# Feed-forward values, residual stream and softmax turned by VectorE and DMA moves in an encoder trunk

## The chip, the cores and the metric

The kernel runs on one core of a Trainium2 chip. The metric is the device time of one execution in microseconds (us), as the median of several runs. All data are float32. The engines of the core are PE (TensorE, matmuls), ACT (ScalarE), DVE (VectorE), POOL (GpSimd) and SP (SyncE, which here only issues DMAs).

## The reference

The input x has 256 tokens of 2048 features; two layers are followed by a last RMSNorm. A layer is:

```python
h    = rms_norm(x, norm1_w)
proj = h @ w_in                       # q, k, v, z, xbc, dt, u
att  = dilated_window_attention(...)  # 3 dilations x 8 slots of 64, merged by their softmax denominators
ssd  = ssd_mixer(...)                 # bidirectional chunked scan, gated, normed: 1024 channels
pool = multiscale_pool(u, ...)        # 512 channels
x    = x + concat(att, ssd, pool) @ w_out
h    = rms_norm(x, norm2_w)
x    = x + (silu(h @ w_gate) * (h @ w_up)) @ w_down     # 5632 inner features
```

## The kernel before

**Units.** The weights (one long array, wall) are cut into 421 units of at most 128x2048 floats, 1 MB. The main loop goes over the units, one step for each. A unit is either of the feature kind (mm_feature: weights stationary, the result has features on the partitions: dt, xbc, q and k, u) or of the token kind (mm_token: the activations stationary, the result has tokens on the partitions: z, v, out, gate, up, down). A token result of 512 columns takes four units (q = 0 to 3), a down result as many as the part has blocks.

**Precision.** Each product is made of float32r pairs. prep splits a weight half (128x1024) into hi (ACT cast, L148) and lo (DVE, L149); the activations are kept as such pairs too (tiles xp, mix, ffp). A token unit has 24 matmuls of 512 columns on PE.

**Order.** All is issued in an order written out by hand, and each engine executes its instructions in that order. In step i SP issues the load of unit i+2 (`load(i + RAW_AHEAD)`, three raw buffers); then the work planned for position "a" is issued; then ACT and DVE prepare the halves 2i+3 and 2i+4 (unit i+1's second and unit i+2's first; five buffers for halves, so a half's buffer is free when PE has used the half five before it); then the work at "b"; then evac takes the result of unit i-1; then the work at "c"; then PE's matmuls of unit i, between which the work planned for a position k of 0 to 15 is put (run_side, side_slot). In a token unit the positions 4kk to 4kk+3 all come at the start of the group kk. `at(step, fn, ..., pos=...)` plans a piece of work.

**What is turned today.** PE turns a 128x128 piece by an instruction of its own, into a PSUM bank, from which ACT and DVE take it. Three places of this kind are touched:

- ff_trans: the feed-forward values (tokens on the partitions), eight transposes for each of 11 blocks of 512 features in a layer, into the pairs ffp (features on the partitions) that the down product reads. Blocks are grouped in parts of 4, 4 and 3 (PARTS); after each part comes its down product.
- xtrans_feat: the residual stream xs after out and after the last down, eight for each of four blocks, into the pairs xp of the next products; three times in the kernel.
- att_b: the softmax (att_a scores and exponent, att_n the scaling), 128x512 for each head slot and token half, eight for a pair and half; att_c multiplies with v. There are four pairs in each layer.

```python
at(b + c, att_a, pair, c, pos=13)
at(b + c + 1, att_n, pair, c, pos="a")
for sl in range(2):
    at(b + c + 1, att_b, pair, sl, c, pos=5)
at(b + c + 2, att_c, pair, c, pos=2)
```

The small transposes of the scan (dt_cols, xtrans, gate2) aren't touched. Tiles t2 are 128x512 (38 buffers), tiles t3 128x768 (8 buffers).

Of the kernel before, what the change touches and what calls it, by code (L numbers as in the profile page):

```python
# [15 lines left out]
F32 = mybir.dt.float32  # L19
F32R = mybir.dt.float32r  # L20
AF = mybir.ActivationFunctionType
ALU = mybir.AluOpType
# [25 lines left out]
def trunk(ctx, tc, xT, xin, wall, par, fin, dsk, plw, cst, dtab, rcnt, out):  # L48
# [22 lines left out]

    def t3(name, dt=F32):
        return ep.tile([128, 3, T], dt, tag="e", name=name)

    def bank(name):
        return auxp.tile([128, 512], F32, tag="aux", name=name)
# [114 lines left out]
    def xpair(k, l, off, v=None):  # L191
# [6 lines left out]
        DVE.scalar_tensor_tensor(t[:, T:], v, w, t[:, :T].bitcast(F32), op0=ALU.mult, op1=ALU.subtract)  # L198
        st["xp"][k] = t

    def residual(n, accs):
        for c in range(2):
            x = xs[c][:, n * 512:n * 512 + 512]
            DVE.tensor_tensor(x, x, accs[c], op=ALU.add)
# [5 lines left out]
            q = t2("sq")  # L210
            ACT.activation(q, xs[c][:, n * 512:n * 512 + 512], AF.Square, accum_out=st["ssq"][:, c * 4 + n:c * 4 + n + 1])

    def xtrans_feat(n, l, off, half):
        p = bank("xf")
        for b in range(2):
            f = (4 * n + 2 * half + b) * 128
            for c in range(2):
                PE.transpose(p[:, b * T + c * 128:b * T + c * 128 + 128], xs[c][:, f:f + 128], ident)  # L218
                yield
        for b in range(2):  # L220
            xpair(4 * n + 2 * half + b, l, off, p[:, b * T:b * T + T])

    def rstd_cols():
        r = sm.tile([128, T + 4], F32, name="rbc", bufs=1)
# [418 lines left out]
    def att_a(pair, c):  # L643
        q, k = st["qk", pair, 0], st["qk", pair, 1]
        p = [bank("sc") for _ in range(2)]
        for o, n, m in ((0, T, 0), (T, 128, 1), (T + 128, 128, 2)):
            for sl in range(2):
                a = slice(64 * sl, 64 * sl + 64)
                PE.matmul(p[sl][:, o:o + n], lhsT=q[a, m, c::2], rhs=k[a, m] if m == 0 else k[a, m, c::2],  # L649
                          start=True, stop=True)  # L650
        if c == 1:
            del st["qk", pair, 0], st["qk", pair, 1]
        for sl in range(2):
            s = t2("s")
            mx = sm.tile([128, 4], F32, tag="mx", name="mx", bufs=6)
            DVE.tensor_tensor_reduce(s, p[sl], dtb[:, c], scale=SLOT_D[2 * pair + sl], scalar=-3e38, op0=ALU.add,  # L656
                                     op1=ALU.max, accum_out=mx[:, 0:1])
            DVE.tensor_scalar(mx[:, 1:2], mx[:, 0:1], -1.0, None, op0=ALU.mult)
            ACT.activation(s, s, AF.Exp, bias=mx[:, 1:2], accum_out=mx[:, 2:3])
            st["p", pair, sl, c] = (s, mx)  # L660

    def att_n(pair, c):
        for sl in range(2):
            s, mx = st["p", pair, sl, c]
            DVE.reciprocal(mx[:, 3:4], mx[:, 2:3])
            DVE.tensor_scalar(s, s, mx[:, 3:4], None, op0=ALU.mult)
            st["p", pair, sl, c] = s

    def att_b(pair, sl, c):
        s = st["p", pair, sl, c]  # L670
        p = bank("pt")
        for b in range(4):
            PE.transpose(p[:, b * 128:b * 128 + 128], s[:, b * 128:b * 128 + 128], ident)  # L673
            yield
        t = t2("pts")
        ACT.copy(t, p)
        st["p", pair, sl, c] = t

    def att_c(pair, c):
        if c == 0:  # L680
            st["op", pair] = bank("op")
        p = st["op", pair]
        pt = [st.pop(("p", pair, sl, c)) for sl in range(2)]
        vs = (st["v", 0, 0], st["v", 0, 1], st["v", 1, c], st["v", 2, c])
        for b in range(4):
            for sl in range(2):
                h = (2 * pair + sl) * 64
                PE.matmul(p[64 * sl:64 * sl + 64, c * 128:c * 128 + 128], lhsT=vs[b][:, h:h + 64],  # L688
                          rhs=pt[sl][:, b * 128:b * 128 + 128], start=(b == 0), stop=(b == 3))
        del pt  # L690
        if c == 0:
            return
        del st["op", pair]
        t = t2("mix", F32R)
        pv = p[:, :T].rearrange("p (c j) -> p j c", c=2)
        hv = t[:, :T].rearrange("p (j c) -> p j c", c=2)
        lv = t[:, T:].rearrange("p (j c) -> p j c", c=2)
        ACT.copy(hv, pv)
        DVE.tensor_tensor(lv, pv, hv.bitcast(F32), op=ALU.subtract)
        st["mix"][MIX_ATT[pair]] = t  # L700
        if pair == 3:
            for g in range(3):
                for c in range(2):
                    del st["v", g, c]
# [41 lines left out]
    def ff_up(f, accs):  # L746
        st["fv"] = []
        for c in range(2):
            v = t2("fv")
            DVE.scalar_tensor_tensor(v, accs[c], st["r"][:, T + c:T + c + 1], st["sg"][c], op0=ALU.mult, op1=ALU.mult)  # L750
            st["fv"].append(v)
        del st["sg"]

    def ff_trans(f, half, fv):
        p = bank("ft")
        for b in range(2):
            o = (2 * half + b) * 128
            for c in range(2):
                PE.transpose(p[:, b * T + c * 128:b * T + c * 128 + 128], fv[c][:, o:o + 128], ident)  # L759
                yield  # L760
        for b in range(2):
            t = t2("ffp", F32R)
            v = p[:, b * T:b * T + T]
            ACT.copy(t[:, :T], v)
            DVE.tensor_tensor(t[:, T:], v, t[:, :T].bitcast(F32), op=ALU.subtract)
            st["ff", 4 * f + 2 * half + b] = t

    def fin_load():
        st["fw"] = [t2("fw") for _ in range(4)]
# [27 lines left out]
    def evac(i, acc):  # L797
# [43 lines left out]
        elif kind == "v":  # L841
            if j % 4 == 3:
                v_evac(j // 4, acc)
        elif kind == "qk":
            pair, m = divmod(j, 6)
            qk_evac(pair, m, acc)
            if m == 5:
                b = i + 3 if pair == 0 else i + 2
                for c in range(2):
                    at(b + c, att_a, pair, c, pos=13)  # L850
                    at(b + c + 1, att_n, pair, c, pos="a")
                    for sl in range(2):
                        at(b + c + 1, att_b, pair, sl, c, pos=5)
                    at(b + c + 2, att_c, pair, c, pos=2)
        elif kind == "u":
            if j == 3:
                pass
            pool_evac(j, acc)
            at(i + 2, pool_mm, l, j, pos=11)
        elif kind == "out":  # L860
            residual(j, acc)
            squares(j)
            at(i + 2, xtrans_feat, j, l, P_N2, 0, pos=2)
            at(i + 2, xtrans_feat, j, l, P_N2, 1, pos=10)
            if j == 3:
                at(i + 3, rstd_cols, pos="b")
        elif kind == "gate":
            st["sg"] = []
            for c in range(2):
                s = t2("sg")  # L870
                ACT.activation(s, acc[c], AF.Silu, scale=st["r"][:, T + c:T + c + 1])
                st["sg"].append(s)
        elif kind == "up":
            ff_up(j, acc)
            fv = st.pop("fv")
            at(i + 2, ff_trans, j, 0, fv, pos=2)
            at(i + 2, ff_trans, j, 1, fv, pos=10)
        elif kind == "down":
            residual(j, acc)
            if u["part"] == len(PARTS) - 1:  # L880
                squares(j)
                if l + 1 < L:
                    at(i + 2, xtrans_feat, j, l + 1, P_N1, 0, pos=2)
                    at(i + 2, xtrans_feat, j, l + 1, P_N1, 1, pos=10)
                    if j == 3:
                        at(i + 3, rstd_cols, pos="b")
                        at(i + 4, rstd_rows, pos=2)
                        at(i + 5, rstd_parity, pos=2)
                else:
                    if j == 0:  # L890
                        ACT.activation(warm, epst, AF.Sqrt)
                        fin_load()
                    if j < 3:
                        fin_weight(j)
            if j == 3:
                for f in range(4 * u["f0"], 4 * (u["f0"] + u["nq"])):
                    del st["ff", f]
# [51 lines left out]
def _constants():  # L949
# [18 lines left out]
    s = np.arange(T)  # L968
    n = [np.minimum(s + w // 2, T) - np.maximum(s - w // 2, 0) for w in (2, 4, 8, 16)]
    rc = (1.0 / np.stack(n)).astype(np.float32).reshape(2, 512)  # L970
    return c, d.astype(np.float32), rc


def _feature(w):
# [9 lines left out]
def _pack(inp):  # L984
    out = []
    put = lambda a: out.append(np.ascontiguousarray(a).reshape(-1))
    for l in range(L):
        w = inp["w_in"][l]
        q, k, v, z, xbc, dt, u = np.split(w, np.cumsum([ATT, ATT, ATT, INNER, 1536, 32])[:6], axis=1)
        put(_token(z))  # L990
        dtp = np.zeros((D, 128), np.float32)
# [18 lines left out]
        for n in range(HELD):  # L1010
            put(o[n][3])
        put(o[HELD:])
        g, up = _token(inp["w_gate"][l]), _token(inp["w_up"][l])
        gu = np.stack([g, up], axis=1)
        f0 = 0
        for n in PARTS:
            put(gu[f0:f0 + n])
            put(_token(inp["w_down"][l][f0 * 512:(f0 + n) * 512]))
            f0 += n
    return np.concatenate(out)  # L1020

# [36 lines left out]
```

## Time and profile before

| | |
|---|---|
| median of 3 runs | 2465.73 us (2465.63 to 2467.09) |
| the profiled execution: its time | 2464.96 us |
| its span, from the first to the last instruction | 2463.2 us |
| PE busy | 2440.2 us, 99% of the span |
| DVE, ACT, POOL busy | 1427.1, 1186.4, 238.1 us (58%, 48%, 10%) |
| mean granted TensorE clock | 0.998 of full speed |
| DMA moved | 458.57 MB, 186 GB/s over the span |

PE's busy time counts latencies of overlapping instructions, so the cost of one matmul is read from the distance of starts. In the rows L149 is line 149 of the kernel; "out<-in" are the program's names; SPq is SP's queue of DMA issues.

### The profile page before, as it was taken

The numbers are of one execution on the slowest core, as the hardware profiler recorded it, in microseconds if no ns is written. First come the engines' busy times: TensorE is split into PE (matmuls) and PEld (weight loads), VectorE is DVE, ScalarE is ACT, GpSimd is POOL, SyncE is SP. The second block draws the span as 40 slices with busy tenths as digits, with TensorE's granted clock in tenths as the row PEclk, the third lists the DMA queues.
The fourth block names the chain that finished last, engine by engine and source line by source line (L and its number), as shares of the span: only waits on it lengthen the run. The fifth ranks groups of instructions, "written<-read, shape, count | busy, mean of one in ns | idle before, by whom it ended". The sixth has DMA issues, their size and how long they took to land.

```text
span 2463.2 us, 30214 instructions
## 1 busy us (share of the span) xinstructions
PE 2440.2 (99%) x11954; PEld 2029.4 (82%) x11954; DVE 1427.1 (58%) x1791; ACT 1186.4 (48%) x1610; POOL 238.1 (10%) x329
## 2 busy tenths in 40 slices
PE   8999999999999999999999999999999999999997
PEld 7888888888888888888888888888888888888886
DVE  6787765555454555545558787655545545454454
ACT  6576554544444444344555755445544444444443
POOL 2175002000000000000001830020000000000001
PEclk9999999999999999999999999999999999999999
DMA  7565544455555555555454654445555555555553
GB/s 271 200 220 171 175 153 155 172 204 188 188 188 196 193 185 194 189 188 190 173 201 157 225 180 155 165 160 188 187 190 188 188 193 187 194 193 191 188 200 125
DMA packets 67103, 458.57 MB, mean 186 GB/s; under 512 B 7776, under 2 KB 7920, under 8 KB 13328
## 3 DMA queue, kind: packets, MB, share of 16 engines
q1 hardware_dynamic: 63360, 445.27, 50.6%
q0 software_dynamic: 3456, 11.09, 1.6%
q8 instruction: 94, 1.54, 0.3%
q14 instruction: 49, 0.40, 0.0%
q10 hardware_dynamic: 144, 0.26, 0.0%
HBM read 454.43 MB, written 2.16 MB: 185 GB/s over the span
## 4 chain that ended last, share of the span: by engine, by line
PE 98%; DVE 1%; ACT 0%; issue 0%; DMA 0%; POOL 0%; SPq 0%; DVEq 0%; ACTq 0%; POOLq 0%
PE acc L321 25%; PE acc L324 25%; PE acc L322 25%; PE acc L286 11%; PE acc L288 6%; PE ft L759 1%; PE acc L291 1%; PE sc L649 1%; PE op L688 1%; PE pt L673 1%; PE y L569 0%; PE y L567 0%; PE xf L218 0%; DMA raw<-wall 0%; DVE s L656 0%
## 5 line engine op out<-in xcount | busy, mean ns | idle before, releaser
L149 DVE TENSOR_TENSOR wlo<-raw,whi 128x1024 fp32r<-128x1024 f32 (+1 forms) x839 | 1028.0, 1234 | 846.9 <-ACT whi L148 845.7
L148 ACT CAST whi<-raw 128x1024 fp32r<-128x1024 f32 (+1 forms) x839 | 873.5, 1049 | 976.9 <-PE acc L324 832.9
L321 PE MATMUL acc<-whi,xp 128*128 128x512 f32 x1728 | 685.8, 397 | 8.4 <-ACT whi L148 8.4
L324 PE MATMUL acc<-whi,xp 128*128 128x512 f32 x1728 | 685.5, 397 | 0.0
L322 PE MATMUL acc<-wlo,xp 128*128 128x512 f32 x1728 | 674.8, 391 | 0.0
L286 PE MATMUL acc<-xp,whi 128*128 128x512 f32 x1230 | 458.3, 409 | 0.0
L321 PEld LDWEIGHTS acc<-whi,xp 128*128 128x128 f32 x1728 | 326.0, 189 | 77.5 <-ACT whi L148 8.4
L324 PEld LDWEIGHTS acc<-whi,xp 128*128 128x128 f32 x1728 | 326.0, 189 | 70.9
L322 PEld LDWEIGHTS acc<-wlo,xp 128*128 128x128 f32 x1728 | 326.2, 189 | 63.6 <-DVE wlo L149 0.4
L288 PE MATMUL acc<-xp,wlo 128*128 128x256 f32 x1312 | 367.2, 290 | 0.0
L324 PE MATMUL acc<-whi,ffp 128*128 128x512 f32 x704 | 277.3, 394 | 0.0
L321 PE MATMUL acc<-whi,ffp 128*128 128x512 f32 x704 | 277.3, 394 | 0.0
L322 PE MATMUL acc<-wlo,ffp 128*128 128x512 f32 x704 | 274.1, 389 | 0.0
L286 PEld LDWEIGHTS acc<-xp,whi 128*128 128x128 f32 x1230 | 231.3, 188 | 50.4 <-issue 3.2
L288 PEld LDWEIGHTS acc<-xp,wlo 128*128 128x128 f32 x1312 | 248.2, 189 | 14.5 <-issue 0.8
L324 PEld LDWEIGHTS acc<-whi,ffp 128*128 128x128 f32 x704 | 132.2, 188 | 29.5
L321 PEld LDWEIGHTS acc<-whi,ffp 128*128 128x128 f32 x704 | 132.2, 188 | 28.6
L322 PEld LDWEIGHTS acc<-wlo,ffp 128*128 128x128 f32 x704 | 132.3, 188 | 26.2
L451 POOL TENSOR_TENSOR pad<-cd,rbc 128x256 f32<-128x256 f32 x24 | 18.7, 781 | 1019.8 <-DVE cd L274 1019.8
L324 PE MATMUL acc<-whi,mix 128*128 128x512 f32 x256 | 102.7, 401 | 0.0
L321 PE MATMUL acc<-whi,mix 128*128 128x512 f32 x256 | 102.1, 399 | 0.0
L322 PE MATMUL acc<-wlo,mix 128*128 128x512 f32 x256 | 99.8, 390 | 0.0
(183 smaller groups left out, 1584.1 us busy)
## 6 DMA issues: line engine op xcount, KB each, us to landing
raw<-wall SPq DMA_DIRECT2D x417, 1024.0 KB, 4.8
rowb<-rowd POOLq DMA_DIRECT2D x32, 256.0 KB, 3.7
xt<-xT SPq DMA_DIRECT2D x8, 256.0 KB, 7.7
xs<-xin SPq DMA_DIRECT2D x2, 1024.0 KB, 7.9
out<-xs SPq DMA_DIRECT2D x5, 256.0 KB, 3.4
raw<-wall SPq DMA_DIRECT2D x4, 256.0 KB, 5.9
rc<-rcnt POOLq DMA_DIRECT2D x4, 256.0 KB, 5.8
fw<-fin POOLq DMA_DIRECT2D x4, 256.0 KB, 3.6
```

Of the source, the lines that this page charges most:

```text
L148: ACT.copy(hi[:, c:e], r)
L149: DVE.tensor_tensor(lo[:, c:e], r, hi[:, c:e].bitcast(F32), op=ALU.subtract)
L286: PE.matmul(acc, lhsT=hi, rhs=rhs, start=first, stop=False)
L288: PE.matmul(acc[:, T:], lhsT=lo, rhs=rhs[:, :T], start=False, stop=False)
L291: PE.matmul(acc, lhsT=hi, rhs=rhs, start=False, stop=True)
L321: PE.matmul(a, lhsT=xh, rhs=hi[:, s], start=first, stop=False)
L322: PE.matmul(a, lhsT=xh, rhs=lo[:, s], start=False, stop=False)
L324: PE.matmul(a, lhsT=xl, rhs=hi[:, s], start=False, stop=last)
L649: PE.matmul(p[sl][:, o:o + n], lhsT=q[a, m, c::2], rhs=k[a, m] if m == 0 else k[a, m, c::2], start=True, stop=True)
L673: PE.transpose(p[:, b * 128:b * 128 + 128], s[:, b * 128:b * 128 + 128], ident)
L688: PE.matmul(p[64 * sl:64 * sl + 64, c * 128:c * 128 + 128], lhsT=vs[b][:, h:h + 64], rhs=pt[sl][:, b * 128:b * 128 + 128], start=(b == 0), ...
L759: PE.transpose(p[:, b * T + c * 128:b * T + c * 128 + 128], fv[c][:, o:o + 128], ident)
```

## The change

The three kinds of PE transposes are taken out. In their place VectorE turns a 128x512 block in 32x32 pieces (each piece in its place), and 16 DMAs on SP's queue, each 32 partitions by 128 columns, move the pieces between the partition groups (`move`). The order of features within 512 is permuted by this; the rows of w_in, w_gate, w_up and w_down, the two norm weights, the transposed input and the distance table are permuted on the host to fit, and the scores are written to PSUM in the permuted order. The hi and lo parts are then taken from the moved tile in SBUF with a strided view (`turned`), one 128x128 piece at a time, so each of these lines has twice as many instructions of half the size. The moves are issued at position "a" two steps after the unit that made the values; the splits stand at positions 2 and 8 of the same step; att_b moves to the step of att_c, and att_c from position 2 to 10.

```diff
+    def move(v, d):
+        for a in range(4):
+            for b in range(4):
+                nc.sync.dma_start(d[32 * b:32 * b + 32, 128 * a:128 * a + 128],
+                                  v[32 * a:32 * a + 32, 128 * b:128 * b + 128])
+
+    def turned(d, m):
+        return d.rearrange("p (a m j) -> p m a j", a=4, m=4)[:, m]
...
-    def xtrans_feat(n, l, off, half):
-        p = bank("xf")
-        for b in range(2):
-            f = (4 * n + 2 * half + b) * 128
+    def x_turn(n):
+        st["xv", n] = [t3f("xv") for _ in range(2)]
+        for c in range(2):
+            DVE.transpose(st["xv", n][c], xs[c][:, n * 512:n * 512 + 512])
+
+    def x_move(n):
+        st["xd", n] = [t2("xd") for _ in range(2)]
+        for v, d in zip(st.pop(("xv", n)), st["xd", n]):
+            move(v, d)
+
+    def x_split(n, l, off, half):
...
+        for m in (2 * half, 2 * half + 1):
+            k = 4 * n + m
+            t = t2("xp", F32R)
+            w = pr[:, l, off + k:off + k + 1]
             for c in range(2):
-                PE.transpose(p[:, b * T + c * 128:b * T + c * 128 + 128], xs[c][:, f:f + 128], ident)
-                yield
-        for b in range(2):
-            xpair(4 * n + 2 * half + b, l, off, p[:, b * T:b * T + T])
+                v = turned(st["xd", n][c], m)
+                hi, lo = (cols(t[:, o + c * 128:o + c * 128 + 128]) for o in (0, T))
+                ACT.activation(hi, v, AF.Copy, scale=w)
+                DVE.scalar_tensor_tensor(lo, v, w, hi.bitcast(F32), op0=ALU.mult, op1=ALU.subtract)
+            st["xp"][k] = t
...
-        for o, n, m in ((0, T, 0), (T, 128, 1), (T + 128, 128, 2)):
+        for o, n, m in ((0, 2, 0), (2, 1, 1), (3, 1, 2)):
...
-                PE.matmul(p[sl][:, o:o + n], lhsT=q[a, m, c::2], rhs=k[a, m] if m == 0 else k[a, m, c::2],
-                          start=True, stop=True)
+                PE.matmul(p[sl].rearrange("p (b m i) -> p m b i", b=4, m=4)[:, o:o + n], lhsT=q[a, m, c::2],
+                          rhs=k[a, m] if m == 0 else k[a, m, c::2], start=True, stop=True)
...
             DVE.tensor_scalar(s, s, mx[:, 3:4], None, op0=ALU.mult)
+            DVE.transpose(s, s)
...
-    def att_b(pair, sl, c):
-        s = st["p", pair, sl, c]
-        p = bank("pt")
-        for b in range(4):
-            PE.transpose(p[:, b * 128:b * 128 + 128], s[:, b * 128:b * 128 + 128], ident)
-            yield
-        t = t2("pts")
-        ACT.copy(t, p)
-        st["p", pair, sl, c] = t
+    def att_b(pair, c):
+        for sl in range(2):
+            d = t3f("pts")
+            move(st["p", pair, sl, c], d)
+            st["p", pair, sl, c] = d
...
-            st["fv"].append(v)
+            t = t3f("ft")
+            DVE.transpose(t, v)
+            st["fv"].append(t)
...
+    def ff_move(f):
+        st["fd"] = [t2("fd") for _ in range(2)]
+        for v, d in zip(st.pop("fv"), st["fd"]):
+            move(v, d)
...
-                    for sl in range(2):
-                        at(b + c + 1, att_b, pair, sl, c, pos=5)
-                    at(b + c + 2, att_c, pair, c, pos=2)
+                    at(b + c + 2, att_b, pair, c, pos="a")
+                    at(b + c + 2, att_c, pair, c, pos=10)
...
-            at(i + 2, ff_trans, j, 0, fv, pos=2)
-            at(i + 2, ff_trans, j, 1, fv, pos=10)
+            at(i + 2, ff_move, j, pos="a")
+            at(i + 2, ff_split, j, 0, pos=2)
+            at(i + 2, ff_split, j, 1, pos=8)
```

ff_split is built as x_split, without the weight; x_turn is called behind squares, x_move and x_split are planned as ff_move and ff_split are.

## Rows read from the trace of the kernel before

**Rows 1.** The profile's page: first line of the chain that ended last.

```profile
PE 98%; DVE 1%; ACT 0%; issue 0%; DMA 0%; POOL 0%; SPq 0%; DVEq 0%; ACTq 0%; POOLq 0%
```

**Rows 2.** Groups by line and form: count, busy us, mean ns, idle before.

```profile
L759 PE MATMUL ft<-cs,fv 128*128 128x128 f32 x176 | 47.7, 271 | 0.0
...
L673 PE MATMUL pt<-cs,s 128*128 128x128 f32 x128 | 32.3, 273 | 1.8 <-DVE s L666 1.8
...
L218 PE MATMUL xf<-cs,xs 128*128 128x128 f32 x96 | 26.0, 271 | 0.0
...
L507 ACT COPY xs<-xt 128x128 f32<-128x128 f32 x16 | 4.1, 256 | 6.1 <-PE xt L504 6.1
```

**Rows 3.** Timeline of PE, starts of three gate units: start us, us.

```profile
903.45 0.39 PE L321 MATMUL acc<-whi,xp 128*128 128x512 f32 x1
...
909.86 0.39 PE L321 MATMUL acc<-whi,xp 128*128 128x512 f32 x1
...
915.30 0.39 PE L321 MATMUL acc<-whi,xp 128*128 128x512 f32 x1
```

**Rows 4.** Timeline of PE, last matmuls of feature units in the attention, and att_c.

```profile
300.72 0.40 PE L291 MATMUL acc<-xp,whi 128*128 128x512 f32 x1
...
307.67 0.40 PE L291 MATMUL acc<-xp,whi 128*128 128x512 f32 x1
...
315.48 0.40 PE L291 MATMUL acc<-xp,whi 128*128 128x512 f32 x1
...
316.50 1.09 PE L688 MATMUL op<-pts,v 128*64 128x128 f32 x16
```

**Rows 5.** Timeline of DVE: the scaling of the softmax.

```profile
308.81 0.49 DVE L666 TENSOR_SCALAR s<-s,mx 128x512 f32<-128x512 f32 x1
```

**Rows 6.** Timeline of DVE and ACT after an up block.

```profile
900.43 1.40 DVE L750 SCALAR_TENSOR_TENSOR fv<-acc,rbc,sg 128x512 f32<-128x512 f32 x2
...
904.73 1.23 DVE L149 TENSOR_TENSOR wlo<-raw,whi 128x1024 fp32r<-128x1024 f32 x1 [1.49 <-ACT whi L148]
...
903.64 1.05 ACT L148 CAST whi<-raw 128x1024 fp32r<-128x1024 f32 x1 [1.66 <-PE acc L324]
```

**Rows 7.** Timeline of SP's queue at the start.

```profile
2.12 1.85 SPq L131 DMA_DIRECT2D raw<-wall  x4
4.02 0.91 SPq L158 DMA_DIRECT2D xt<-xT  x2
...
5.55 2.53 SPq L158 DMA_DIRECT2D xt<-xT  x2
```

**Rows 8.** Issues of the weight loads: duration ns, least, median, most.

```profile
L133 SPq DMA_DIRECT2D raw<-wall x417: 327/328/538, 5.0 to 2425.3; - x139
```

**Rows 9.** DMA issues: count, KB each, median us to landing.

```profile
raw<-wall SPq DMA_DIRECT2D x417, 1024.0 KB, 4.8
...
raw<-wall SPq DMA_DIRECT2D x4, 256.0 KB, 5.9
...
pr<-par SPq DMA_DIRECT2D x1, 118.0 KB, 2.1
```

**Rows 10.** Waits of SP's queue: us in total, times, longest.

```profile
SPq L158 <- DMA raw<-wall: 1.9, 2, 1.4
```

**Rows 11.** Timeline of PE and DVE in the out product.

```profile
447.40 0.39 PE L321 MATMUL acc<-whi,mix 128*128 128x512 f32 x1
...
449.83 1.28 DVE L204 TENSOR_TENSOR xs<-xs,acc 128x512 f32<-128x512 f32 x2
```

**Rows 12.** Timeline of PE's first matmuls; two windows at the end (after POOL: clock).

```profile
8.43 0.80 PE L321 MATMUL acc<-whi,xp 128*128 128x512 f32 x1 [8.43 <-ACT whi L148]
...
14.44 0.61 PE L322 MATMUL acc<-wlo,xp 128*128 128x512 f32 x1
...
2450.00:2451.00 1.00, 0.46 (x3) 0.03 (x1) 1.00 (x2) 0.46 (x1) 0.00 (x0) 1.00 0.00 0
2455.00:2456.00 1.00, 0.00 (x0) 0.00 (x0) 0.17 (x1) 1.00 (x3) 0.00 (x0) 0.72 0.80 277
```

More of the change, by code (lines that the diff above doesn't have):

```diff
@@ L73, in t3, with t3f @@
         return ep.tile([128, 3, T], dt, tag="e", name=name)
+    def t3f(name):
+        return t3(name).rearrange("p a b -> p (a b)")[:, :512]
     def bank(name):
@@ L199, in xpair, with cols @@
         st["xp"][k] = t
+    def move(v, d):
[5 more added lines that the diff above has]
+        return d.rearrange("p (a m j) -> p m a j", a=4, m=4)[:, m]
+    def cols(t):
+        return t.rearrange("p (a j) -> p a j", a=4)
     def residual(n, accs):
@@ L211, in squares @@
             ACT.activation(q, xs[c][:, n * 512:n * 512 + 512], AF.Square, accum_out=st["ssq"][:, c * 4 + n:c * 4 + n + 1])
-    def xtrans_feat(n, l, off, half):
-        p = bank("xf")
-        for b in range(2):
-            f = (4 * n + 2 * half + b) * 128
-            for c in range(2):
-                PE.transpose(p[:, b * T + c * 128:b * T + c * 128 + 128], xs[c][:, f:f + 128], ident)
-                yield
-        for b in range(2):
-            xpair(4 * n + 2 * half + b, l, off, p[:, b * T:b * T + T])
+    def x_turn(n):
[7 more added lines that the diff above has]
+    def x_split(n, l, off, half):
+        if n == 0 and half == 0:
+            st["xp"] = [None] * KT
+        for m in (2 * half, 2 * half + 1):
+            k = 4 * n + m
+            t = t2("xp", F32R)
+            w = pr[:, l, off + k:off + k + 1]
+            for c in range(2):
+                v = turned(st["xd", n][c], m)
[3 more added lines that the diff above has]
+            st["xp"][k] = t
+        if half:
+            del st["xd", n]
     def rstd_cols():
@@ L688, in att_c @@
                 PE.matmul(p[64 * sl:64 * sl + 64, c * 128:c * 128 + 128], lhsT=vs[b][:, h:h + 64],
-                          rhs=pt[sl][:, b * 128:b * 128 + 128], start=(b == 0), stop=(b == 3))
+                          rhs=turned(pt[sl], b), start=(b == 0), stop=(b == 3))
         del pt
@@ L750, in ff_up, with ff_split @@
             DVE.scalar_tensor_tensor(v, accs[c], st["r"][:, T + c:T + c + 1], st["sg"][c], op0=ALU.mult, op1=ALU.mult)
-            st["fv"].append(v)
+            t = t3f("ft")
+            DVE.transpose(t, v)
+            st["fv"].append(t)
         del st["sg"]
[L754 to L757, printed above, removed]
-            for c in range(2):
[L759 to L766, printed above, removed]
+    def ff_move(f):
+        st["fd"] = [t2("fd") for _ in range(2)]
+        for v, d in zip(st.pop("fv"), st["fd"]):
+            move(v, d)
+    def ff_split(f, half):
+        for m in (2 * half, 2 * half + 1):
+            t = t2("ffp", F32R)
+            for c in range(2):
+                v = turned(st["fd"][c], m)
+                hi, lo = (cols(t[:, o + c * 128:o + c * 128 + 128]) for o in (0, T))
+                ACT.copy(hi, v)
+                DVE.tensor_tensor(lo, v, hi.bitcast(F32), op=ALU.subtract)
+            st["ff", 4 * f + m] = t
+        if half:
+            del st["fd"]
     def fin_load():
@@ L862, in evac @@
             squares(j)
-            at(i + 2, xtrans_feat, j, l, P_N2, 0, pos=2)
-            at(i + 2, xtrans_feat, j, l, P_N2, 1, pos=10)
+            x_turn(j)
+            at(i + 2, x_move, j, pos="a")
+            at(i + 2, x_split, j, l, P_N2, 0, pos=2)
+            at(i + 2, x_split, j, l, P_N2, 1, pos=8)
             if j == 3:
@@ L874, in evac @@
             ff_up(j, acc)
-            fv = st.pop("fv")
-            at(i + 2, ff_trans, j, 0, fv, pos=2)
-            at(i + 2, ff_trans, j, 1, fv, pos=10)
+            at(i + 2, ff_move, j, pos="a")
+            at(i + 2, ff_split, j, 0, pos=2)
+            at(i + 2, ff_split, j, 1, pos=8)
         elif kind == "down":
@@ L882, in evac @@
                 if l + 1 < L:
-                    at(i + 2, xtrans_feat, j, l + 1, P_N1, 0, pos=2)
-                    at(i + 2, xtrans_feat, j, l + 1, P_N1, 1, pos=10)
+                    x_turn(j)
+                    at(i + 2, x_move, j, pos="a")
+                    at(i + 2, x_split, j, l + 1, P_N1, 0, pos=2)
+                    at(i + 2, x_split, j, l + 1, P_N1, 1, pos=8)
                     if j == 3:
@@ L970, in _constants, with _order @@
     rc = (1.0 / np.stack(n)).astype(np.float32).reshape(2, 512)
+    d = d.reshape(128, 2, 4, 4, 32).transpose(0, 1, 3, 2, 4).reshape(128, 2, 512)
     return c, d.astype(np.float32), rc
+def _order(n):
+    f = np.arange(n).reshape(n // 512, 4, 4, 32)
+    return f.transpose(0, 2, 1, 3).reshape(n)
 def _feature(w):
@@ L987, in _pack @@
     for l in range(L):
-        w = inp["w_in"][l]
+        w = inp["w_in"][l][_order(D)]
         q, k, v, z, xbc, dt, u = np.split(w, np.cumsum([ATT, ATT, ATT, INNER, 1536, 32])[:6], axis=1)
@@ L1012, in _pack @@
         put(o[HELD:])
-        g, up = _token(inp["w_gate"][l]), _token(inp["w_up"][l])
+        g, up = _token(inp["w_gate"][l][_order(D)]), _token(inp["w_up"][l][_order(D)])
         gu = np.stack([g, up], axis=1)
@@ L1017, in _pack @@
             put(gu[f0:f0 + n])
-            put(_token(inp["w_down"][l][f0 * 512:(f0 + n) * 512]))
+            put(_token(inp["w_down"][l][f0 * 512:(f0 + n) * 512][_order(n * 512)]))
             f0 += n
@@ L1032, in cols @@
             return a.reshape(-1, 128).T
-        par[:, l, P_N1:P_N1 + 16] = cols(inp["norm1_w"][l])
-        par[:, l, P_N2:P_N2 + 16] = cols(inp["norm2_w"][l])
+        par[:, l, P_N1:P_N1 + 16] = cols(inp["norm1_w"][l][_order(D)])
+        par[:, l, P_N2:P_N2 + 16] = cols(inp["norm2_w"][l][_order(D)])
         par[:, l, P_CW:P_CW + 60] = inp["conv_w"][l].reshape(5, 12, 128).transpose(2, 1, 0).reshape(128, 60)
@@ L1043 @@
     arrays = dict(
-        xT=np.ascontiguousarray(inp["x"][0].reshape(T, KT, 128).transpose(2, 1, 0)),
+        xT=np.ascontiguousarray(inp["x"][0][:, _order(D)].reshape(T, KT, 128).transpose(2, 1, 0)),
         xin=inp["x"][0].reshape(2, 128, D), wall=wall, par=par,
```

## The prediction

> **What bounds the kernel now.** The chain that ended last comes first. It is PE for 98% of the span [rows 1]: the reader is to see that no wait of any length is on it, so every PE instruction taken out is time won, and every wait that PE gets is time lost. The groups by line and form say next what the edit can take out: the three transposing lines hold 176, 128 and 96 instructions of 128x128, each shown at 0.27 us [rows 2]. That duration is a latency; what one costs PE has to be read from starts in the timeline. A feed-forward unit that carries eight of them runs from 903.45 to 909.86, 6.41 us, and the next, without any, to 915.30, 5.44 us [rows 3]. Eight cost 0.97 us. In the attention the ends of two feature units lie 6.95 us apart when the second unit has the scores alone, and 7.81 us when it has the scores and eight transposes [rows 4]: 0.86 us for eight.
>
> **What is removed.** 176 transposes are 22 units of eight, 96 are 12, at 0.97 us: 21.3 and 11.6 us. 128 are 16 units at 0.86 us: 13.8 us. Together 46.7 us come off PE. With the PSUM banks go the ACT copies of the transposed softmax, which hide under PE either way. If nothing else came, 2464.96 - 46.7 = 2418 us.
>
> **What is added on VectorE and ScalarE.** 100 block transposes of 128x512. No row shows one; the nearest, a 128x512 DVE pass from SBUF to SBUF, takes 0.49 us [rows 5], and the 128x512 product from PSUM 0.70 (1.40 for two) [rows 6]. I take 0.6; they only delay the moves. A half-size split costs on ACT about what the 128x128 copy does, 0.256 us [rows 2], and at most twice that; I take 0.3, so eight ACT parts of one 512-column block are 2.4 us, and 0.3 more until DVE has followed. Strided reads by PE and its strided score writes I cost at nothing: the number of columns stays.
>
> **What is added on SP.** Each block of 128x512 becomes 16 DMAs of 16 KB, each pair of blocks a set of 32. There are 22 sets for the feed-forward values, 16 for the softmax, 12 for the residual stream: 50 sets, 1600 DMAs, on the one queue that also issues the weight loads, in program order. What an issue costs is the term on which all hangs. In the opening burst four pieces of raw start at 2.12 and the next load at 4.02 [rows 7]: 0.475 us from one to the next, 0.46 busy (1.85 for four), though a piece has only 256 KB. The 417 weight loads, each issued alone, show 0.327 us at least and 0.328 in the middle [rows 8]. So the price is per instruction: 0.46 in a row, bounds 0.33 (a set is 10.6 us) and 0.475; I take 0.46, because a set is such a burst: 14.7 us. A 16 KB transfer by itself is nothing: at the 4.8 us of a 1 MB weight load [rows 9] it is 0.08 us. For landing I take 2.0 us, by the 118 KB transfer that landed in 2.1 us [rows 9]; bounds 0 and 4.8 us, that of the weight load. A second limit shows in the same burst: the second of the two loads from 5.55 on, the twelfth DMA of the queue, goes out at about 7.7 us [rows 7], when the fourth, the first piece of raw, had landed (2.12 and some 5.9) [rows 9], and SP is shown waiting for a raw landing on the line that loads xt [rows 10]. Eight DMAs are outstanding at most. With 2 us of landing this doesn't bind (8 x 0.46 = 3.7 us), but behind a weight load it does: the eighth DMA after it waits for its 4.8 us, 1.1 us more than its issues take.
>
> The Trainium skill, in "DMA: Bandwidth & Descriptors", section "Issuing engines are not separate DMA queues", says that the issuing time on a sequencer is usually small relative to the DMA itself. The rows contradict it for pieces this small: 0.46 us of issue against 0.08 us of transfer. By the rule a set would cost about 2.5 us and the sum would be the 2418 us of the second rival below.
>
> **Feed-forward, 22 sets.** Take the unit after an up block in the trace. The two values are made at 900.43 [rows 6]; the first is turned by about 901.75. SP then issues until 916.45, and the set has landed at 918.45. Meanwhile ACT is in the next step's program: it made the cast at 903.64 [rows 6], the first half of the weights of the unit two later, and stands at the first split. Behind the split on ACT and DVE stand all later casts and lo parts; PE waits for those. Without transposes PE's units start at 903.45, 908.89, 914.33, and it runs out of prepared weights in the middle of the third, at 917.05. The splits take ACT 2.4 us from 918.45, the cast 1.05, the lo part 1.23 [rows 6], and PE has one matmul (0.23) before it needs lo: it goes on at 922.9. Stall 5.9 us, for the 16 blocks that more blocks follow. The next weight load, queued behind the set, lands at about 921.7, just in time for the cast after; so the load is late but covered. For the last block of a part the down product reads the split: splits ready at 921.2 against 914.33 where the part has four blocks (6.8 us, 4 times), against 908.89 where it has three (12.3 us, twice). Sum 94 + 27 + 25 = 146 us.
>
> **Softmax, 16 sets in 8 pairs.** Count from the start of the step after the scores (307.9). The first half is scaled by 309.3 [rows 5], turned by 309.9: t = 2.0. The set lands at 2.0 + 14.7 + 2.0 = 18.7. PE comes to the products with v, now at position 10 of 16 of the following unit, at 6.95 + 3.55 = 10.5; PE is in order, so everything waits behind it: 8.2 us. The second set starts after the first and one weight load (17.2), ends at 33.0 with the 1.1 us of the limit, lands at 35.0; PE is there at 18.7 + 1.1 [rows 4] + 2.1 + 3.55 = 25.5, stall 9.5. A pair 17.7 us, eight pairs 142 us.
>
> **Residual stream, 12 sets.** In a step that starts at 447.4 the two sums are finished at 451.1 [rows 11], the first block is turned 4.4 us into the step. The feed-forward argument gives 6.5 us for a set, 7.5 for the last of four (its splits are read by the fourth unit on). In the out product the first two blocks end in consecutive units, so the second set queues behind the first: it ends at 35.4, PE goes on at 41.9 and would have needed it at 31.0: 10.9 us. An out phase makes 6.5 + 10.9 + 6.5 + 7.5 = 31.4, two 63; the passage to layer 2 makes 3 x 6.5 + 7.5 = 27. Sum 90 us.
>
> **PE's clock.** After its 8.4 us of waiting PE's matmuls of 512 columns, 15 from 8.43 to 14.44, start 0.43 us apart [rows 12], against 0.227 later (24 in 5.44 us) [rows 3]: 15 at half pace cost 3.0 us. At the end PE's last matmul lies in 2450 to 2451, and the mean granted clock is 1.00 there and 0.72 in 2455 to 2456 [rows 12], so it fell to the 1.2 GHz level about 5 us after PE stopped. Nothing in between shows a stall. I charge 3.0 us to each stall clearly longer than that which has no later one of the same chain to hide it: 8 in the softmax (the second of a pair), 6 at part ends, 2 and 3 in the residual stream; 57 us. Bounds: none, and all 42 (another 69 us).
>
> **Sum.** 146 + 142 + 90 + 57 - 46.7 = +388 us on the profiled execution's 2464.96 (span 2463.2), 2853; the median of the runs lies 0.8 us above that execution, so 2855 us. With 0.43 us for an issue (48 us less) and no clock loss 2748, with the clock loss everywhere 2922.
>
> **The rivals.**
> Cheaper issue. A DMA of 32 rows may cost the 0.33 us of a lone issue [rows 8]. A set is then 10.6 us, and the same sums give 54 + 83 + 42 = 179 us, less 46.7: 2597 us, with stalls mostly too short for the clock. For it: the 0.33 was measured with SP otherwise idle, and these have a quarter of the rows. Against it: the bursts.
> Everything hidden, faster. If an issue takes under 0.20 us, the softmax set lands before position 10 (10.5 - 4.0 = 6.5 us for 32), the feed-forward set before ACT is late (8.8 us needed), and the 46.7 us stay: 2418 us. The place is SP's queue alone; at some 0.25 us the stalls in the softmax and at the part ends eat the gain. Against it: none of the 417 issues took less than 0.327 us [rows 8].
> Landing binds. If pieces written from SBUF to SBUF, with weight loads about, land like those loads in 4.8 us, eight outstanding mean 0.6 us for each; a set is 19.2 us, 4.5 us more for each of 50: about 3080 us.
> No net effect: an issue price by chance near 0.25 us, 2465 us.
>
> **Chances.** Forecast (2748 to 2922) 0.60; cheaper issue 0.18; landing binds 0.14; hidden 0.06; no effect 0.02. The likeliest is 2855. 2570 to 2950 takes in the first two cases with their bounds and the near edge of the third; 2 in 10 stay outside. A measurement of this kernel tells 0.2% (5 us) from no change. Faster 0.06, same 0.01, slower 0.93.
>
> **What would show it.** PE's share of the chain falls to about 85%, and DMA and SP stand on it; the waits show PE's op product for the moved softmax and ACT's splits for moved blocks, some 5 to 10 us each; SP's queue shows bursts of 32 at 0.46 us; weight loads are issued in clumps behind them; the granted clock dips in the attention. No PE transposes under the three lines. Wrong it would be if the bursts run at 0.2 us, if the splits don't hold up the casts behind them, or if the queue is limited by landing.

## The result and the profile after

The changed kernel takes 3109.15 us against 2465.76 us: 1.2607 times the time before, 95% interval 1.2585 to 1.2629. The forecast was slower, 2855 us, in a range up to 2950: the sign and the place are right, the size is 643 us where 389 were forecast, and the time lies above the range.

The page of the kernel after, its first engine line, the granted clock in 40 slices, and the first line of the chain that ended last; they answer to [rows 1]:

```profile
PE 2526.2 (81%) x11554; PEld 2074.4 (67%) x11554; DVE 1493.4 (48%) x2027; ACT 1180.1 (38%) x1714; POOL 235.2 (8%) x329
...
PEclk9999788889899989998889997779799899989998
...
PE 55%; SPq 28%; DMA 5%; DVE 5%; ACT 3%; issue 3%; POOL 0%; ACTq 0%; DVEq 0%; POOLq 0%
```

400 instructions have left PE (11954 to 11554), and yet PE is busy 86 us longer; it stands idle for 579 us, and SP's queue, which had no share of the chain, holds 28% of it; PE's share fell to 55%, where the prediction had about 85%. The waits of PE (total us, times, longest) name what it stands for:

```profile
PE acc L353 <- ACT whi L152: 255.4, 26, 12.8
PE op L717 <- DMA pts<-s: 195.4, 31, 9.9
PE acc L353 <- ACT ffp L796: 61.9, 8, 9.2
PE acc L353 <- ACT xp L249: 22.4, 4, 9.5
```

These are the places of the prediction: the weights not yet prepared, the product with v, the last splits of a part, and those of the residual stream. The issues behind them, by the feed-forward instructions of the moving line (ns: least, median, most), and the median time from issue to landing (us):

```profile
L208 SPq DMA_DIRECT2D fd<-ft x704: 507/589/1725, 709.2 to 3034.5; - x176
```

```profile
fd<-ft SPq DMA_DIRECT2D x704, 16.0 KB, 1.8
```

Against the 0.328 us of a weight load [rows 8] a move takes 0.589 us of SP, and it lands in 1.8 us. One feed-forward set, the last of a part of four blocks, in the timelines of SP and ACT:

```profile
1188.45 20.21 SPq L208 DMA_DIRECT2D fd<-ft  x32
1208.76 11.41 SPq L137 DMA_DIRECT2D raw<-wall  x5
...
1190.10 1.06 ACT L152 CAST whi<-raw 128x1024 fp32r<-128x1024 f32 x1 [1.67 <-PE acc L356]
1199.72 0.30 ACT L796 CAST ffp<-fd 128x128 fp32r<-128x128 f32 x1 [8.57 <-DMA fd<-ft]
1209.91 1.50 ACT L796 CAST ffp<-fd 128x128 fp32r<-128x128 f32 x7 [9.88 <-DMA fd<-ft]
1211.31 1.04 ACT L152 CAST whi<-raw 128x1024 fp32r<-128x1024 f32 x1
```

The 32 moves take 20.2 us, 0.63 from start to start, where [rows 7] had given 0.475. The first half-size split waits for the first block's moves, the second for the other block's, and ACT casts no weight between 1191.2 and 1211.3. Behind the set five weight loads follow in a clump. PE at the end of that stall, and windows around it (us, then the busy time of each engine; after POOL: the granted clock):

```profile
1210.26 0.79 PE L353 MATMUL acc<-whi,ffp 128*128 128x512 f32 x1 [8.64 <-ACT ffp L796]
1210.85 0.63 PE L354 MATMUL acc<-wlo,ffp 128*128 128x512 f32 x1
...
1213.84 0.61 PE L356 MATMUL acc<-whi,ffp 128*128 128x512 f32 x1
1214.26 0.41 PE L353 MATMUL acc<-whi,ffp 128*128 128x512 f32 x1
```

```profile
1203.00:1205.00 2.00, 0.00 (x0) 0.00 (x0) 0.00 (x0) 0.00 (x0) 0.00 (x0) 0.76 0.13 29
...
1211.00:1213.00 2.00, 2.00 (x7) 1.52 (x6) 1.36 (x5) 1.35 (x4) 0.00 (x0) 0.50 0.99 418
...
1215.00:1217.00 2.00, 2.00 (x10) 1.67 (x9) 2.00 (x2) 1.52 (x2) 0.00 (x0) 1.00 0.99 360
```

The clock fell while PE stood, and after 8.6 us of standing PE's first nine matmuls run at the 1.2 GHz level, to about 1214.2: some 2 us more, on top of the stall itself.

### The profile page after: what moved, and what is told of

Its sections match the earlier page's. It is cut to its first block, busy times and chain, and to the rows that moved or that the text cites. A ratio compares the mean times of both kernels' runs of the same rounds, so it can differ in the third digit from the quotient of the medians.

```text
span 3105.1 us, 32148 instructions
## 1 busy us (share of the span) xinstructions
PE 2526.2 (81%) x11554; PEld 2074.4 (67%) x11554; DVE 1493.4 (48%) x2027; ACT 1180.1 (38%) x1714; POOL 235.2 (8%) x329
## 4 chain that ended last, share of the span: by engine, by line
PE 55%; SPq 28%; DMA 5%; DVE 5%; ACT 3%; issue 3%; POOL 0%; ACTq 0%; DVEq 0%; POOLq 0%
SPq L208 28%; PE acc L354 14%; PE acc L356 14%; PE acc L353 14%; PE acc L318 7%; PE acc L320 4%; DMA raw<-wall 3%; DVE wlo L153 2%; ACT whi L152 2%; DMA fd<-ft 1%; DMA pts<-s 1%; ACT ffp L796 1%; DVE ft L781 1%; PE op L717 1%; DVE fv L779 0%
## 5 line engine op out<-in xcount | busy, mean ns | idle before, releaser
L353 PE MATMUL acc<-whi,xp 128*128 128x512 f32 x1728 | 700.4, 405 | 188.3 <-ACT whi L152 165.8
L354 PE MATMUL acc<-wlo,xp 128*128 128x512 f32 x1728 | 693.4, 401 | 8.3 <-DVE wlo L153 8.3
L356 PE MATMUL acc<-whi,xp 128*128 128x512 f32 x1728 | 693.1, 401 | 0.0
L353 PEld LDWEIGHTS acc<-whi,xp 128*128 128x128 f32 x1728 | 336.9, 195 | 267.0 <-ACT whi L152 172.9
L354 PEld LDWEIGHTS acc<-wlo,xp 128*128 128x128 f32 x1728 | 336.2, 195 | 86.7 <-DVE wlo L153 18.2
L356 PEld LDWEIGHTS acc<-whi,xp 128*128 128x128 f32 x1728 | 335.9, 194 | 69.5
L797 DVE TENSOR_TENSOR ffp<-fd,ffp 128x128 fp32r<-128x128 f32 x176 | 39.5, 287 | 393.0 <-ACT ffp L796 376.0
L353 PEld LDWEIGHTS acc<-whi,ffp 128*128 128x128 f32 x704 | 136.4, 194 | 119.7 <-ACT ffp L796 66.8
L717 PE MATMUL op<-pts,v 128*64 128x128 f32 x256 | 38.8, 414 | 198.8 <-DMA pts<-s 195.4
L796 ACT CAST ffp<-fd 128x128 fp32r<-128x128 f32 x176 | 39.4, 294 | 413.3 <-DMA fd<-ft 413.3
L717 PEld LDWEIGHTS op<-pts,v 128*64 128x64 f32 x256 | 28.6, 214 | 207.9 <-issue 162.6
L353 PE MATMUL acc<-whi,mix 128*128 128x512 f32 x256 | 107.2, 419 | 66.0 <-ACT whi L152 66.0
```

Of the source, the lines that this page charges most:

```text
L353: PE.matmul(a, lhsT=xh, rhs=hi[:, s], start=first, stop=False)
L354: PE.matmul(a, lhsT=xh, rhs=lo[:, s], start=False, stop=False)
L356: PE.matmul(a, lhsT=xl, rhs=hi[:, s], start=False, stop=last)
L796: ACT.copy(hi, v)
L797: DVE.tensor_tensor(lo, v, hi.bitcast(F32), op=ALU.subtract)
```

## The experiments

Eleven kernels ran, each against the kernel before on the same chip (2464.4 to 2465.5 us there).

**What an issue costs, by itself.** The kernel before, with bursts behind its last output:

```diff
+        for a, b in n16:
+            nc.sync.dma_start(box(d, b, a), box(src, a, b))
...
+        for n in range(16):
+            nc.sync.dma_start(d[:, 32 * n:32 * n + 32], src[:, 32 * n:32 * n + 32])
```

> The kernel before, with bursts of DMAs put behind its last output (nothing reads them): 16 each of 16 KB moves between partition groups, the same without a change of group, 128 partitions by 32 columns, the 32x128 piece and the 128x32 piece from the weights in HBM, the 32x128 piece to HBM; then four of 128x512 within SBUF and four from HBM; then 16 moves on ACT's queue and 16 on POOL's. The disputed size is the 0.63 us from move to move in the changed kernel (0.59 us busy), where I had taken 0.46. If it belongs to the instruction's form, the moves take 0.59 to 0.63 us here too, with no weight load about, and the forms differ: those of 32 rows dearer than those of 128. If it comes from the weight loads and the waits in the changed kernel, all bursts show 0.43 to 0.48 us here. If it belongs to reading SBUF, the three SBUF forms show 0.6 and the HBM ones 0.45.

The timelines of SP, ACT and POOL (pa: moves between partition groups, the last 13 of 16; pb: without a change of group; pc: 128x32; pd and pe: 32x128 and 128x32 from HBM; prd: to HBM; pg and ph: 128x512 within SBUF and from HBM; pi and pj: moves on ACT's queue, the last 11, and on POOL's, the first ten):

```profile
2460.84 8.19 SPq L807 DMA_DIRECT2D pa<-xs  x13
2469.76 10.03 SPq L810 DMA_DIRECT2D pb<-xs  x16
2479.90 10.18 SPq L813 DMA_DIRECT2D pc<-xs  x16
2490.19 7.48 SPq L816 DMA_DIRECT2D pd<-wall  x16
2497.78 7.46 SPq L819 DMA_DIRECT2D pe<-wall  x16
2505.29 7.43 SPq L821 DMA_DIRECT2D prd<-xs  x16
2512.83 2.42 SPq L824 DMA_DIRECT2D pg<-xs  x4
2515.34 2.48 SPq L827 DMA_DIRECT2D ph<-wall  x4
...
2520.74 7.16 ACTq L830 DMA_DIRECT2D pi<-xs  x11
...
2455.60 4.95 POOL L833 DMA_DIRECT2D pj<-xs  x10 [15.12 <-ACT xs L792]
```

Divide by the count: 0.630, 0.627 and 0.636 us for an issue of 16 KB with both ends in SBUF, 0.467, 0.466 and 0.464 with one end in HBM, in either direction. 32 rows or 128 make no difference, nor does the change of group, nor, within SBUF, sixteen times the bytes (pg 0.605). The first three issues of pa, which ran beside POOL's burst, took longer. It isn't the reading of SBUF either: prd reads it too. So none of the three readings offered beforehand holds as it stands: the price goes with both ends. One burst doesn't fit: ph, 256 KB from HBM, takes 0.62 us each, where 256 KB from HBM took 0.475 in [rows 7]. It ran beside ACT's burst; that this is the reason isn't shown. So the 0.46 to 0.475 of [rows 7] was true, of another kind of DMA: every DMA that SP issued in the kernel before had one end in HBM. Why SBUF to SBUF costs 0.16 us more at 16 KB is open.

**No moves.**

```diff
-        st["fd"] = [t2("fd") for _ in range(2)]
-        for v, d in zip(st.pop("fv"), st["fd"]):
-            move(v, d)
+        st["fd"] = st.pop("fv")
```

and the same in x_move and att_b.

> The changed kernel without its 1600 moves: the splits and the products with v read the block that VectorE turned, so the values are out of place; everything else (block turns, half-size splits, strided score writes) is kept. If the moves are the whole loss, this is the kernel before less the 46.7 us of the transposes: 2419 us, range 2412 to 2435, PE 98 to 99% of the span and the granted clock 0.99. If the smaller ACT and DVE pieces or the strided accesses cost PE anything, it lies above 2440 us.

2425.48 us, ratio 0.9837 (0.9821 to 0.9854): 40 us less than before. PE's busy time and its one new wait:

```profile
PE 2395.5 (99%) x11554; PEld 1998.1 (82%) x11554; DVE 1488.6 (61%) x2027; ACT 1182.5 (49%) x1714; POOL 238.8 (10%) x329
```

```profile
PE pl L761 <- POOL pm L755: 7.7, 2, 3.8
```

PE is busy 44.7 us less than in the profile before, and has 7.7 us of new waits for POOL's pooling work, which it now reaches too early. The block turns and the half-size splits cost the path nothing that these rows show. All of the loss is the moves'.

**Moves that nobody reads.** The moves go into two tiles of their own; splits and products read the turned block.

```diff
+    dump = [const.tile([128, 512], F32, name="dump%d" % n) for n in range(2)]
...
+        st["fd"] = st.pop("fv")
+        for v, d in zip(st["fd"], dump):
             move(v, d)
```

(In this run the pool of 128x768 tiles has six buffers in place of eight, to make room.)

> The changed kernel with all 1600 moves on SP's queue, but into two tiles that nothing reads; splits and products read the turned block, as in the run without moves. So nobody waits for a landing, and only the weight loads queue behind the moves. If the wait at the split and at the product with v is what stops PE, nearly all of the loss goes: about 2430 to 2520 us. If the occupied queue is enough by itself (a load behind a set of 20.2 us lands some 25 us after the turn, PE has weights for about 15 to 18 us), the feed-forward and residual sets still cost 5 to 10 us each, and the softmax pairs, two sets in a row, more: 2700 to 2950 us.

3038.84 us, above the highest figure: with nobody reading a moved block, 613 of the 684 us that the moves cost over the run without them stay. (Engines other than PE still wait for buffers that a move is reading: POOL 29.1, ACT 12.7, DVE 12.4 us in all.) SP and ACT around one set:

```profile
1154.88 20.36 SPq L209 DMA_DIRECT2D dump<-ft  x32
1175.33 20.24 SPq L137 DMA_DIRECT2D raw<-wall  x7
...
1157.53 1.69 ACT L795 CAST ffp<-ft 128x128 fp32r<-128x128 f32 x8
...
1180.40 1.99 ACT L152 CAST whi<-raw 128x1024 fp32r<-128x1024 f32 x2 [20.01 <-DMA raw<-wall]
```

The splits are made at once, and ACT then stands 20 us for the next weights: their load was issued at 1175.3, behind the set, and landed at 1180.4. The queue alone is enough.

**All moves from POOL's queue.** `nc.gpsimd` in place of `nc.sync` in move; no weight load stands behind a move any more.

> All moves from POOL's queue, so that no weight load stands behind a move; the waits at the splits and at the product with v stay. POOL issued 16 such moves in 8.0 us behind the last output, 0.5 us each, landing 3.4 us: a set is some 16 us and lands at 19.5. If the late weight loads were the whole loss (the unread moves cost 613 us of it), it goes: 2430 to 2480 us. If the waits hold ACT and PE up as the prediction has it, its sums with a set 1.3 us longer than there and 1.4 us more of landing stay: 2850 to 2950 us.

3000.99 us, above the range of 2850 to 2950, and far from 2480. The timeline of POOL for one set, then PE's waits:

```profile
1156.95 5.86 POOL L208 DMA_DIRECT2D fd<-ft  x12 [36.60 <-DVE fv L779]
1164.31 9.77 POOL L208 DMA_DIRECT2D fd<-ft  x20 [1.51 <-DMA fd<-ft]
```

```profile
PE acc L353 <- ACT whi L152: 194.7, 26, 10.3
PE op L717 <- DMA pts<-s: 176.5, 27, 11.9
```

A set takes 17.1 us here. With no weight load behind the set, the readers' waits for the moved blocks alone cost 576 us over the run without moves. Together with the run before: either path, the late load or the wait at the reader, is enough by itself for nearly the whole loss. They run side by side from the same cause, the length of a set. An estimate by the prediction's times, with a set of 20.2 us: a load issued at 922 lands at 927, and its weights are ready at 929, where PE wants them at 919.8 (2.7 us, the work of a half, after 917.05), some 9.5 us late; the path through the splits is late by 10.6 us.

**Every second move from POOL's queue.**

```diff
-                nc.sync.dma_start(d[32 * b:32 * b + 32, 128 * a:128 * a + 128],
+                (nc.sync if b % 2 else nc.gpsimd).dma_start(d[32 * b:32 * b + 32, 128 * a:128 * a + 128],
```

> The changed kernel with every second move issued from POOL's queue, which is nearly idle. Same moves, same bytes, same waits. If SP's issue rate sets the length of a set, a set takes about 10 us (16 x 0.63) and the sums of the prediction, which give 2597 us for a set of 10.6 us, hold: 2540 to 2680 us. If the landing or the moving of small rows sets it, the time stays at 3000 to 3150 us.

2617.64 us, as it should be if SP's issues set the length of a set. SP's timeline for one set:

```profile
1007.45 10.09 SPq L208 DMA_DIRECT2D fd<-ft  x16
```

Same bytes, same waits, half the length of a set: 492 of the 643 us go.

**The same pieces from HBM.** The test of the mis-sized term: the same count, tiles and waits, but only the first of each 16 DMAs reads the turned block.

```diff
+                s = v if a == b == 0 else units[0]["src"]
                 nc.sync.dma_start(d[32 * b:32 * b + 32, 128 * a:128 * a + 128],
-                                  v[32 * a:32 * a + 32, 128 * b:128 * b + 128])
+                                  s[32 * a:32 * a + 32, 128 * b:128 * b + 128])
```

> The changed kernel with the same 1600 DMAs of 32x128 on SP's queue into the same tiles, with the same waits, but only the first of each 16 reads the turned block; the other 15 read pieces of the weights in HBM, so the values are others. Behind the last output such a piece cost 0.467 us of SP from start to start, a move within SBUF 0.627. If the mis-sized price of an issue is what the prediction lacked, a set is now some 15.3 us (2 x 0.63 + 30 x 0.467), 0.5 us above the 14.7 us that it used, and its sum comes out: 2855 us, 2790 to 2900. If the number of DMAs or their landing makes the loss, it stays at 3050 to 3110 us.

2881.55 us, 27 above the forecast for the changed kernel. SP for one set:

```profile
1104.03 0.51 SPq L209 DMA_DIRECT2D fd<-ft  x1
1104.60 7.07 SPq L209 DMA_DIRECT2D fd<-wall  x15
1111.83 0.51 SPq L209 DMA_DIRECT2D fd<-ft  x1
1112.38 7.08 SPq L209 DMA_DIRECT2D fd<-wall  x15
```

15.4 us for this set in place of 20.2 (15.8 in the middle of the 50), and 228 of the 254 us by which the forecast was missed are gone.

**One part alone.** Feed-forward, softmax, residual stream; the other two parts as in the kernel before, with their weights in the old order.

> Only the feed-forward values are turned by VectorE and moved (22 sets); residual stream and softmax stay with PE. With a set at the 20.2 us that the changed kernel shows and a landing of 1.8 us, the prediction's steps give 16 stalls of 10.6, 4 of 11.5 and 2 of 16.9 us, 3 us of lost clock for each and 21 us of transposes saved: +294 us, 2760 us (2700 to 2800). If the sets hurt each other mainly where they follow closely, as in the softmax, this one costs far less: under 2600 us.

> Only the softmax is turned and moved (16 sets in 8 pairs). By the same steps a pair stalls PE by 13.7 and 14.6 us, 3 us of clock, less 13.8 us in all: +237 us, 2702 us (2650 to 2740). If the next weight loads were what stops PE and not the product with v, the pair would cost less, since the loads behind a pair have four units to catch up: about 2560 us.

> Only the residual stream is turned and moved (12 sets). With a set of 20.2 us the prediction's steps give 50 us for an out phase, twice, and 47 us for the passage to the second layer, some 36 us of lost clock, less 11.6 us of transposes: +171 us, 2636 us. The three parts alone would then add up to the whole: 258 us (feed-forward, measured) + 221 us (softmax, measured) + 165 us = 644 us asks for 2629 us. Below 2600 us or above 2660 us the parts disturb each other.

2722.43, 2685.40 and 2630.22 us: +258, +221 and +166, which add up to 645 us; the whole costs 643. The parts don't disturb each other. The steps of the prediction, with the measured set, gave 294, 237 and 171.

**Out to HBM and back.** One DMA out and one back for a block, and a feature order in which the partition of the moved tile runs on without a break (p = 4i + b), so that 128 partitions go in one DMA:

```diff
+    def out_in(vs, ds):
+        r = [drp.tile([4, 128, 128], F32, name="bnc", bufs=4) for _ in vs]
+        for v, t in zip(vs, r):
+            nc.sync.dma_start(t.rearrange("a (i b) c -> (a i) (b c)", b=4), v)
+        for d, t in zip(ds, r):
+            nc.sync.dma_start(d.rearrange("p (a c) -> p a c", a=4), t.rearrange("a p c -> p a c"))
...
-    return f.transpose(0, 2, 1, 3).reshape(n)
+    return f.transpose(0, 2, 3, 1).reshape(n)
```

> Instead of 16 moves a block goes out to HBM in one DMA of 128x2 KB and comes back in one of 128x4x512 B, with the features in another order: 4 issues for a set in place of 32, at some 0.47 us each (one end in HBM). Landing about 3 us each way by the outputs of 256 KB (2.7 to 3.4 us), and the second block is turned 1.45 us after the first: a set lands some 9 us after the first turn. By the prediction's thresholds (10.8 us for the feed-forward set, 8.4 for the softmax, 7.1 less the splits where a part has three blocks) nearly nothing is left of the stalls: the 2425 us of the run without moves plus some 10 to 15 us, 2438 us (2426 to 2465). If a small number of issues isn't what matters but the traffic or the landing, it is no faster than the kernel before.

2430.72 us, ratio 0.9861 (0.9844 to 0.9877) to the kernel before: faster than both kernels, 5 to 6 us above the run without moves. SP's and ACT's timelines for one set, the landings, and PE's waits:

```profile
929.92 1.71 SPq L208 DMA_DIRECT2D bnc<-ft  x2
932.00 1.81 SPq L210 DMA_DIRECT2D fd<-bnc  x2
933.90 8.94 SPq L137 DMA_DIRECT2D raw<-wall  x4
...
936.46 1.50 ACT L795 CAST ffp<-fd 128x128 fp32r<-128x128 f32 x7 [1.25 <-DMA fd<-bnc]
```

```profile
bnc<-ft SPq DMA_DIRECT2D x44, 256.0 KB, 2.0
fd<-bnc SPq DMA_DIRECT2D x44, 256.0 KB, 2.8
```

```profile
PE rr L267 <- DVE rbc L260: 7.1, 1, 7.1
PE op L717 <- DMA pts<-bnc: 2.1, 5, 0.7
```

SP is free again 4 us after the first turn, and the set has landed after 6.5 us. The Trainium skill, in "DMA: Bandwidth & Descriptors", section "Rules for kernel authors", asks for many small transfers to be put together into large ones, since under 64 KB one pays mostly overhead; these runs agree: 32 issues of 16 KB hold SP for 20.2 us, four of 256 KB for 4.

**The way back on POOL's queue.** `nc.gpsimd` in the second loop of out_in.

> The version through HBM with the way back issued from POOL's queue, so that SP doesn't stand waiting for the way out to land before it issues the next weight load. If SP's hold costs the version through HBM its last 5 us above the run without moves, this one is at 2425 to 2428 us; if the landing is what is left (the product with v waited 2.1 us in all, one wait of 7.1 us at the passage to layer 2), it is the same 2428 to 2435 us; if POOL's own work delays the way back, above 2435 us.

2495.00 us, ratio 1.0116 (1.0099 to 1.0133), above 2435 us and slower than the kernel before. The landings of the feed-forward blocks, and SP and POOL around one set:

```profile
fd<-bnc POOLq DMA_DIRECT2D x44, 256.0 KB, 7.8
```

```profile
942.85 1.71 SPq L208 DMA_DIRECT2D bnc<-ft  x2
944.65 1.01 SPq L137 DMA_DIRECT2D raw<-wall  x2
...
945.40 0.75 POOL L210 DMA_DIRECT2D fd<-bnc  x1 [41.26 <-DMA bnc<-ft]
```

The way back lands after 7.8 us where SP's took 2.8. POOL had stood idle for 41 us before it, so its own work isn't the cause here. The queue isn't the only difference: SP, which no longer waits, sends two weight loads 0.75 us ahead of the way back, where in the run before they went out behind it (933.90 after 932.00). Of the 100 ways back of all three parts, 59 were issued with two weight loads in flight and landed after 7.7 us in the middle, 36 with one after 5.3, and 5 with none after 3.6; from SP's queue all 100 went out with none in flight, and landed after 2.8. So most of the dearer landing goes with the loads ahead of it; what part POOL's queue has in it isn't shown. SP's wait had kept the loads behind the way back.

## Why the prediction was wrong

**Right.** The mechanism: transposes taken from PE are worth their time, the moves cost it back on SP's queue, and PE stands at the product with v, at the splits and at the weights behind them. The landing (taken 2.0 us, measured 1.8) and the block turn (taken 0.6 us, measured 0.71) were near. The limit of eight outstanding DMAs did not bind between moves, 8 x 0.63 = 5.0 us being longer than a landing. The rival with about the right time, 3080 us by late landings, is right by chance: the landing was not late.

**The step that failed** is the price of an issue: "0.46 in a row, bounds 0.33 (a set is 10.6 us) and 0.475". It measured 0.63 us, outside its bounds; a set is 20.2 us and not 14.7, so every stall behind a set was forecast too short. The bounds came from rows of DMAs between HBM and SBUF, and nothing in the trace of before shows one within SBUF. The run with pieces from HBM shows that this term makes up the miss: with issues at 0.47 us the kernel takes 2882 us. The rule of the Trainium skill weighed there ("DMA: Bandwidth & Descriptors", section "Issuing engines are not separate DMA queues"), that issuing is usually small relative to the DMA, was contradicted by more than the prediction thought: 0.63 us of issue against its estimate of 0.08 us of transfer. The range was too narrow at its upper end for the same reason: an operation with no row had been bounded by rows of a different kind.

**The clock**, a second term of the wrong size, was charged for 19 stalls, 57 us, with 126 us for all 42 as its bound. PE's 11554 instructions are busy 2395.5 us in the run without moves and 2526.2 in the changed kernel: 131 us, and 126 us (2521.8) in the run with pieces from HBM. The bound is about what came. The granted clock in the changed kernel's trace shows why: PE stands 50 times for 8.5 to 15.4 us, and each time it goes on at the 1.2 GHz level. It is busy for 242 us at that level, which costs half of them, 121 us; the other 10 us aren't accounted for.

**The stalls** were too large at equal length of a set: forecast 378 us at 14.7 us; in the run with pieces from HBM PE's idle time (span less busy, 357.9 us) exceeds that of the run without moves (28.8) by 329 us, though its sets are longer (15.4 us and more).

**The transposes** were worth 40 us and not 46.7, in part because PE then waits for POOL. At an issue price of 0.47 us the forecast had the stalls 49 us too long, the loss by the clock 69 us too small and the gain from the transposes 7 us too large. In the run with pieces from HBM these errors cancel to 27 us; that its time lies so near the forecast is in part luck.

For the changed kernel the loss divides into idle time 579 - 29 = 550 us and slower work 131 us, less 40 us. (That these add up, to 641 of the 643 us, proves nothing: a span is busy time and idle time.)

**"The load is late but covered"** holds only as the prediction says it, behind a stall that is there anyway. The unread moves show that the load is a second sufficient cause.

## What to carry to other kernels

For 16 KB the price of an issue depended on where both ends of the transfer lie, so a row of one kind is no bound for another; where a queue also feeds the weights, multiply that price by the number of issues in a burst and compare it with what is buffered ahead. When two waits hang on the same burst, taking one away gives almost nothing back; shorten the burst. Here that turned a loss of 643 us into a gain of 34: fewer and larger DMAs, by a data order in which 128 partitions move at once, even over HBM. And look at what a wait on a queue keeps back before taking it out: in the last run the weight loads that it had held went ahead of the urgent transfer.

## What the runs showed of the hardware

- A DMA of 16 KB issued by SP took 0.63 us from start to start with both ends in SBUF, 0.465 us with one in HBM, as 32x128 or as 128x32. At 256 KB it was 0.605 us within SBUF, and from HBM 0.475 us in the opening burst and 0.62 us beside a burst on ACT's queue. A move took 0.65 us on ACT's queue (the last 11 of 16) and 0.495 us on POOL's (the first ten).
- 256 KB back from HBM in rows of 512 B landed after 2.8 us from SP's queue with no weight load in flight at the issue; from POOL's queue after 3.6 us with none (5 cases), 5.3 with one, 7.7 with two.
- VectorE turned a 128x512 float32 block in 32x32 pieces in 0.711 us.
